# A two-layer hybrid block on one Trainium2 core: order of the routing step, arm of the expert branch, and contraction rows of the differential scores

## Chip, cores and metric

The kernel runs on one core of a Trainium2 chip. The metric is the device time of one launch in microseconds. A profiled execution gives a span from its first to its last instruction.

## What is computed

256 latent and 256 context tokens of width 1024 pass through two layers; the output is the latent stream after a last norm. All is 32-bit float. Cut to what matters here:

```python
def diff_attend(q, k, v, lam):                       # 4 heads, two score maps each
    s = jnp.einsum('bqhd,bkhd->bhqk', q, k) * HEAD_DIM ** -0.5     # HEAD_DIM = 64
    p = jax.nn.softmax(s, axis=-1).reshape(b, DIFF_HEADS, 2, nq, nkeys)
    return jnp.einsum('bhqk,bkhd->bqhd', p[:, :, 0] - lam * p[:, :, 1], v)

def moe_ffn(h, w_router, w1, w3, w2):                # layer 1, 8 experts of 3584
    top_vals, top_idx = lax.top_k(h @ w_router, 2)
    top_w = jax.nn.softmax(top_vals, axis=-1)
    gates = jnp.sum(jax.nn.one_hot(top_idx, 8) * top_w[..., None], axis=-2)
    return sum(gates[..., e:e+1] * swiglu(h, w1[e], w3[e], w2[e]) for e in range(8))

# per layer: h = modulate(rms_norm(x)); x += g_a * (concat[neighbourhood attention (4 heads),
#   differential attention, gated short conv] @ w_out); h = modulate(rms_norm(x)); x += g_f * ffn(h)
# ffn: dense SwiGLU in layer 0, moe_ffn in layer 1 (latent tokens alone)
```

## The kernel before

Activations lie transposed in SBUF (`xT`: 8 tiles of 128 features by 512 tokens; columns 256 to 511 are latent). Weights stream in over SP's queue. For the wide products a weight chunk is split into a high and a low part in fp32r (ACT writes `whi`, DVE `wlo`), and three matmuls replace one (`mm3`, lines 222 to 224).

**Mixers.** `proj_kq` projects one pair of neighbourhood heads (names `na 0`, `na 1`) or one differential head (`df 0` to `df 3`, with `rotate` set) and splits keys and queries. A score map has 64 contraction rows; `ks` and `qs` pack the high part of the keys and their low part into 128 rows, and `ql` holds the low part of the queries, one map in rows 0 to 63 and the other in rows 64 to 127. `scores` takes, for each query tile, two 128-row matmuls (line 560) and two 64-row ones (line 563); the moving side is 512 keys for latent queries, 256 for context ones. The attention itself is written as generators that two lanes step through while projections are emitted (`pace`, `step`); `finish` steps until the named heads are all emitted. The tile framework then sets each engine's order. The bias of the neighbourhood heads lies in two buffers of a pool, filled by 16 small loads a layer and masked by `mask_bias` (lines 715 and 716), on DVE for `na 0` and on GpSimd (POOL) for `na 1`.

**Routing.** After layer 1's output projection, `route` takes the norm's factor `r`, the top two experts of each token, the tokens' places in each expert (`by`, `pp`), the experts' sizes and an integer `few` for the branch. GpSimd multiplies `xT` by the norm (line 1327), ACT scales and shifts it (line 1330, the normed latents `hT`), TensorE transposes it (line 1337) into token rows `hk`, and a one-hot product gathers the rows of expert 7 from `hk` into `x7` (lines 1343 to 1347). `first_steps` then emits eight steps of expert 7 ahead of the branch: 32-column products into PSUM tiles `L` (line 1619), each step four weight chunks, with folds through PSUM tile `tg` (line 1640).

**Branch.** `moe_main` tests `few > 64`. The general arm is the larger part of the program and stands first; the data here take the other arm, which runs experts 0 and 1 as "heavy" (PSUM tiles `H`) and the others as "light" in an interleaving that a table of costs sets. Line 1903 holds the program's end and its barriers.

Of the kernel before, what the change touches and what calls it, by code (L numbers as in the profile page):

```python
# [13 lines left out]
F32 = mybir.dt.float32  # L14
F32R = mybir.dt.float32r
I32 = mybir.dt.int32
U32 = mybir.dt.uint32
# [6 lines left out]
KT = 8  # L24
# [105 lines left out]
def tile_hybrid_block(ctx: ExitStack, tc: tile.TileContext, x, c, cx, c_ctx, ada_w, ada_b, w_in, w_out, na_rpb,  # L130
# [357 lines left out]
    def proj_kq(l, name, rotate, ps=None):  # L488

        ap = st["apool"]  # L490
        q0 = 256 * l
        if ps is not None:
            pk, pq = ps
        elif l == 0:
            pk, pq = project(0, 512)
        else:
            ps = [bank("mm"), bank("mm", (128, 256))]
            for u in range(2):
                wh, wl = ws.next()
                wh = wh.rearrange("p (k n) -> p k n", k=4)  # L500
                wl = wl.rearrange("p (k n) -> p k n", k=4)
                for k in range(4):
                    kt = 4 * u + k
                    for i, a in ((0, 0), (1, 256)):
                        cs = slice(i * 128, (i + 1) * 128)
                        mm3(ps[i], wh[:, k, cs], wl[:, k, cs], hb["h"][:, kt, a:], hb["l"][:, kt, a:],
                            kt == 0, kt == KT - 1)
                    pace()
            pk, pq = ps
        units = [("na", 0), ("na", 1)] + [("df", j) for j in range(4)]  # L510
        finish(*units[:max(0, units.index(name) - 2)])

        ks = [ap.tile([128, 512], F32R, name="ks", tag="ks", bufs=6) for _ in range(2)]
        qs = [ap.tile([128, 512 - q0], F32R, name="qs", tag="qs", bufs=6) for _ in range(2)]
        ql = ap.tile([128, 512 - q0], F32R, name="ql", tag="ql", bufs=3)

        def rows_of(v):
            return v.rearrange("p (r n) -> p r n", n=GW)

        def key_parts(src, a):  # L520
            for m in range(2):
                r, o = slice(64 * m, 64 * m + 64), slice(64 - 64 * m, 128 - 64 * m)
                cs = slice(a, a + src.shape[1])
                act.activation(ks[m][r, cs], src[r], AF.Copy)
                dve.tensor_tensor(out=ks[m][o, cs], in0=src[r], in1=ks[m][r, cs].bitcast(F32), op=ALU.subtract)

        def query_parts(src, a):
            src, (hs, low) = rows_of(src), [[rows_of(q[:, a:a + src.shape[1]]) for q in qq] for qq in (qs, [ql])]
            if not rotate:

                src = src[:, :, ::-1]
            for m in range(2):
                r, o = slice(64 * m, 64 * m + 64), slice(64 - 64 * m, 128 - 64 * m)
                for h in (r, o):
                    act.activation(hs[m][h], src[r], AF.Copy, scale=0.125)
                dve.scalar_tensor_tensor(out=low[0][r], in0=src[r], scalar=0.125, in1=hs[m][r].bitcast(F32),
                                         op0=ALU.mult, op1=ALU.subtract)
        if rotate:
            uk = rope(pk[:, 256:512])
            key_parts(pk[:, :256], 0)  # L540
            uq = rope(pq[:, 256 - q0:512 - q0])
            if l == 0:
                query_parts(pq[:, :256], 0)
            key_parts(uk, 256)
            query_parts(uq, 256 - q0)
        else:
            key_parts(pk, 0)
            query_parts(pq, 0)
        st[name] = (ks, qs, ql)

    def scores(ln, kq, grp, qt, bias=None):

        ks, qs, ql = kq
        nk = 256 if grp == 0 else 512
        q0 = 256 * grp + 128 * qt - st["t0"]
        q = slice(q0, q0 + 128)
        s = [bank(f"at{ln}", (128, nk)) for _ in range(2)]
        kw = dict(skip_group_check=True)
        for m in range(2):
            pe.matmul(s[m], qs[m][:, q], ks[m][:, :nk], start=True, stop=False, **kw)  # L560
        for m in range(2):
            r = slice(64 * m, 64 * m + 64)
            pe.matmul(s[m], ql[r, q], ks[m][r, :nk], start=False, stop=True, **kw)
        if bias is not None:
            for m in range(2):
                dve.tensor_tensor(out=s[m][:, 256:], in0=s[m][:, 256:], in1=bias[m], op=ALU.add)
        return s
# [655 lines left out]
    def route():  # L1223
# [16 lines left out]
        for t in range(2):  # L1240
            for h in range(2):
# [1 line left out]
                for k in range(4):  # L1243
                    pe.transpose(p[:, k, :], xT[:, 4 * h + k, 256 + t * 128:384 + t * 128], ident)
                act.activation(xk[t][:, 4 * h:4 * h + 4, :], p, AF.Copy)
        bc = bank("mm", (128, 256))
        for t in range(2):
            pe.matmul(bc[:, t * 128:t * 128 + 128], r[:, t:t + 1].to_broadcast([128, 128]), ident, start=True,
                      stop=True)

        mo["g"] = mp.tile([128, 28 * 64], F32, name="g")
        bcs = mo["g"][:, :256]
        act.copy(bcs, bc)
        ls = mp.tile([128, 2, NE], F32, name="ls")

        by = mp.tile([128, 6, NE], F32, name="by")
        for t in range(2):
            dve.scalar_tensor_tensor(out=ls[:, t, :], in0=mo["lg"][:, t, :], scalar=r[:, t:t + 1], in1=mo["rb"],
                                     op0=ALU.mult, op1=ALU.add)
        tops, ms = [], []  # L1260
        for t in range(2):
            top, idx, idf = sm(8), sm(8, U32), sm(8)
            dve.max(out=top, in_=ls[:, t, :])
            dve.max_index(out=idx, in_max=top, in_values=ls[:, t, :])
            dve.tensor_copy(idf, idx)
            m0, m1 = sm(8), sm(8)
            dve.tensor_scalar(out=m0, in0=iota[:, :NE], scalar1=idf[:, 0:1], scalar2=None, op0=ALU.is_equal)
            dve.tensor_scalar(out=m1, in0=iota[:, :NE], scalar1=idf[:, 1:2], scalar2=None, op0=ALU.is_equal)
            dve.tensor_tensor(out=by[:, t, :], in0=m0, in1=m1, op=ALU.add)
            tops.append(top)  # L1270
            ms.append((m0, m1))
        pc = bank("at1", (128, NE))
        for t in range(2):
            pe.matmul(pc, mo["ones"], by[:, t, :], start=(t == 0), stop=(t == 1))
        pp = bank("at1", (128, 2, NE))
        pe.matmul(pp[:, 0, :], mo["before"], by[:, 0, :], start=True, stop=True)
        pe.matmul(pp[:, 1, :], mo["ones"], by[:, 0, :], start=True, stop=False)
        pe.matmul(pp[:, 1, :], mo["before"], by[:, 1, :], start=False, stop=True)
        gf = mo["gf"] = mp.tile([128, KT, 128], F32, name="gf")
        for h in range(2):  # L1280
            p = bank("mm", (128, 4, 128))
# [18 lines left out]
        mo["few"] = nc.values_load(ints[0:1, 2, 0:1], min_val=0, max_val=128 * 256)  # L1300
        dve.tensor_copy(sidf, sidx)
        for t in range(2):
            top, (m0, m1), g = tops[t], ms[t], sm(8)
            dve.tensor_scalar(out=g[:, 0:1], in0=top[:, 0:1], scalar1=-1.0, scalar2=None, op0=ALU.mult)
            act.activation(g[:, 1:2], top[:, 1:2], AF.Exp, bias=g[:, 0:1])
            dve.tensor_scalar(out=g[:, 2:3], in0=g[:, 1:2], scalar1=1.0, scalar2=None, op0=ALU.add)
# [2 lines left out]
            dve.tensor_scalar(out=by[:, 2 + t, :], in0=m1, scalar1=g[:, 4:5], scalar2=None, op0=ALU.mult)  # L1309
            dve.scalar_tensor_tensor(out=by[:, 2 + t, :], in0=m0, scalar=g[:, 3:4], in1=by[:, 2 + t, :],  # L1310
                                     op0=ALU.mult, op1=ALU.add)
        dve.tensor_copy(by[:, 4:6, :], pp)
        sel = mp.tile([128, 2, 32], F32, name="sel0")
        one_hot(sel, 0, iota[:, :32], by)

        pm = mp.tile([128, NE, NE], F32, name="pm")
        dve.tensor_tensor(out=pm, in0=iota[:, None, :NE].to_broadcast([128, NE, NE]),
# [4 lines left out]
            dve.tensor_tensor(out=pd[:, i], in0=by[:, i, None, :].to_broadcast([128, NE, NE]), in1=pm, op=ALU.mult)  # L1322
        dve.reduce_sum(out=rk, in_=pd, axis=AX.X)

        hT = mo["hT"] = xT[:, :, 256:512]
        for k in range(0, KT, 2):
            gp.tensor_tensor(out=hT[:, k:k + 2, :], in0=hT[:, k:k + 2, :],
                             in1=bcs[:, None, :].to_broadcast([128, 2, 256]), op=ALU.mult)
            for kt in (k, k + 1):
                act.activation(hT[:, kt, :], hT[:, kt, :], AF.Identity, bias=mods[1][:, 24 + kt, 1:2],  # L1330
                               scale=mods[1][:, 32 + kt, 1:2])
        hk = mo["hk"] = mp.tile([128, 2, D], F32, name="hk")
        for h in range(2):
            for t in range(2):
                p = bank("mm", (128, 4, 128))
                for k in range(4):
                    pe.transpose(p[:, k, :], hT[:, 4 * h + k, t * 128:(t + 1) * 128], ident)
                (act.copy if t else dve.tensor_copy)(hk[:, t, h * 512:(h + 1) * 512], p.rearrange("p a b -> p (a b)"))

        p = bank("mm", (128, KT, 32))  # L1340
        for t in range(2):
            for c in range(4):
                pe.matmul(p[32 * c:32 * c + 32], sel[:, t, :],
                          hk[:, t, :].rearrange("p (k c i) -> p c k i", c=4, i=32)[:, c], start=(t == 0),
                          stop=(t == 1), tile_position=(0, 32 * c), skip_group_check=True)
        x7 = mp.tile([128, KT, 32], F32, name="x7")
        dve.transpose(out=x7, in_=p)
        dstack["psum"].close()
        mo["psum"] = stack(tc.tile_pool(name="psum_m", bufs=1, space=PSUM))
        mo["rows"], mo["e"], mo["ring"] = Rows(), {}, deque()  # L1350
        mo["rows"].v["x"] = x7
        mo["fg"] = xT[:, :, 384:512]
# [12 lines left out]
        mo["left"], mo["early"] = mo["early"], {}  # L1365

    def pbank(tag):
        return mo["psum"].tile([128, 512], F32, name=tag, tag=tag, bufs={"H": 4, "L": 2, "tg": 2}[tag])

    def weights(w, r, row0, c0, nk):  # L1370

# [454 lines left out]
    def moe_main():  # L1826
        route()
        first_steps()
        with tc.If(mo["few"] > 64) as more:
            moe_general()  # L1830
        with more.Else():
            mix_experts([0, 1], [((7,), 32), ((2,), 64), ((3, 4, 5), 32)], begun=True)
# [74 lines left out]
```

## Time and profile before

| what | us |
|---|---|
| median of 3 runs | 1706.23 (1705.69 to 1714.27) |
| profiled execution, own time | 1709.09 |
| its span | 1707.3 |
| TensorE busy in it | 1639.5 (96%) |
| VectorE (DVE) / ScalarE (ACT) / GpSimd busy | 1030.1 / 639.0 / 17.6 |

TensorE is PE in the rows, its weight loads PEld. Mixer 0 lies at about 60 to 290 us of the span, the dense part up to 720, mixer 1 up to 878, routing and the first steps up to 914, the taken arm up to 1703. A matmul's busy time overlaps the next one's; what a matmul costs is read from one start to the next. A row of a window gives its start and end, its length, the busy time of PE, PEld, DVE, ACT and POOL (with the number of instructions), then TensorE's granted clock as a share of full speed, the busy share of the DMA engines, and GB/s. A row of a timeline gives start, duration, engine, line, operation, its result and inputs and their tile, size, the number of instructions joined in it, and in brackets the idle time ahead of it with what ended that.

### The profile page before, as it was taken

Reading aid. Unit: us, or ns where it says so; the run is one execution under the profiler, and the core shown is the slowest. Engines: PE = TensorE matmul, PEld = TensorE weight load, DVE = VectorE, ACT = ScalarE, POOL = GpSimd, SP = SyncE. Lnnn points to the kernel's source line nnn. Section 1 sums busy time; section 2 is a strip of 40 time slices with the busy share of each in tenths; the row PEclk is TensorE's granted clock in tenths of the full one; section 3 lists DMA queues with packets and bytes.
Section 4 is the critical chain, followed back from the end, with each engine's and each line's share of the span. In section 5 each row is a group of like instructions: output and inputs, shape, how many; then the busy total and the mean of one; then the engine's idle time right before and its main releaser. Section 6 shows DMA issues by size and latency. Waiting matters only on the chain. (4 is left out here: it accounts for less than half of the span.)

```text
span 1707.3 us, 28490 instructions
## 1 busy us (share of the span) xinstructions
PE 1639.5 (96%) x10942; PEld 1265.7 (74%) x10942; DVE 1030.1 (60%) x2043; ACT 639.0 (37%) x1057; POOL 17.6 (1%) x27
## 2 busy tenths in 40 slices
PE   7999999999999999999987999999999999999996
PEld 4777778988878888988772766676787686868773
DVE  4778877888877884788862353124454535354454
ACT  4555444422212232555533322222343234433341
POOL 0101000000000000000010000000000000000000
PEclk9999999999999999999988999999999999999999
DMA  9744343256555453352498999989999999999995
GB/s 287 179 132 111 99 149 99 88 185 197 197 169 171 154 185 111 99 149 75 162 355 312 409 380 340 349 332 401 360 368 398 364 353 364 405 386 350 388 381 193
DMA packets 234193, 434.66 MB, mean 255 GB/s; under 512 B 23496, under 2 KB 142784, under 8 KB 234048
## 3 DMA queue, kind: packets, MB, share of 16 engines
q1 hardware_dynamic: 232560, 432.14, 71.2%
q8 instruction: 88, 1.44, 0.3%
q10 hardware_dynamic: 1488, 0.62, 0.1%
q14 instruction: 57, 0.47, 0.1%
HBM read 431.66 MB, written 1.05 MB: 253 GB/s over the span
## 5 line engine op out<-in xcount | busy, mean ns | idle before, releaser
L471 DVE TENSOR_TENSOR wlo<-raw,whi 128x1024 fp32r<-128x1024 f32 x168 | 202.9, 1223 | 234.2 <-ACT whi L469 221.5
L222 PE MATMUL H<-xh,whi 128*128 128x256 f32 x896 | 257.2, 287 | 2.6 <-ACT whi L469 1.8
L224 PE MATMUL H<-xh,wlo 128*128 128x256 f32 x896 | 254.5, 284 | 2.0 <-DVE wlo L471 1.9
L223 PE MATMUL H<-xl,whi 128*128 128x256 f32 x896 | 254.1, 284 | 0.0
L469 ACT ACTIVATE whi<-raw 128x1024 fp32r<-128x1024 f32 x168 | 174.3, 1054 | 180.4 <-PE H L223 86.3
L222 PE MATMUL mm<-hh,whi 128*128 128x512 f32 (+1 forms) x648 | 230.4, 356 | 2.4 <-ACT hh L469 1.7
L223 PE MATMUL mm<-hl,whi 128*128 128x512 f32 (+1 forms) x648 | 225.8, 349 | 0.0
L224 PE MATMUL mm<-hh,wlo 128*128 128x512 f32 (+1 forms) x648 | 225.7, 349 | 0.0
L100 ACT ACTIVATE whi<-raw 128x1024 fp32r<-128x1024 f32 x130 | 134.3, 1055 | 241.4 <-DMA raw<-in_ffn_w_dram 128.2
L101 DVE TENSOR_TENSOR wlo<-raw,whi 128x1024 fp32r<-128x1024 f32 x130 | 157.0, 1221 | 60.1 <-ACT whi L100 59.3
L222 PEld LDWEIGHTS H<-xh,whi 128*128 128x128 f32 x896 | 172.3, 192 | 20.0 <-issue 9.3
L224 PEld LDWEIGHTS H<-xh,wlo 128*128 128x128 f32 x896 | 172.4, 192 | 3.0 <-DVE wlo L471 3.0
L223 PEld LDWEIGHTS H<-xl,whi 128*128 128x128 f32 x896 | 172.4, 192 | 0.2
L222 PEld LDWEIGHTS mm<-hh,whi 128*128 128x128 f32 x648 | 122.9, 190 | 22.5 <-issue 4.0
L1619 PE MATMUL L<-raw,xT 128*32 128x512 f32 (+1 forms) x896 | 137.2, 597 | 0.3
L224 PEld LDWEIGHTS mm<-hh,wlo 128*128 128x128 f32 x648 | 122.9, 190 | 16.7 <-issue 2.1
L223 PEld LDWEIGHTS mm<-hl,whi 128*128 128x128 f32 x648 | 123.3, 190 | 13.7 <-issue 0.5
L322 DVE SCALAR_TENSOR_TENSOR ada_t<-raw,scol,ada_t 128x256 f32<-128x256 f32 x266 | 116.6, 482 | 2.8
L1632 ACT ACTIVATE s<-L 128x512 f32<-128x512 f32 x70 | 41.8, 597 | 152.6 <-PE L L1619 127.2
L222 PE MATMUL H<-whi,gh 128*128 128x512 f32 x224 | 90.0, 402 | 3.9 <-ACT gh L469 3.1
L1644 DVE STREAM_TRANSPOSE sT<-tg 128x128 f32<-128x128 f32 x56 | 15.5, 308 | 129.4 <-PE tg L1640 129.3
L223 PE MATMUL H<-wlo,gh 128*128 128x512 f32 x224 | 88.8, 396 | 0.9 <-DVE wlo L471 0.9
(312 smaller groups left out, 2754.1 us busy)
## 6 DMA issues: line engine op xcount, KB each, us to landing
raw<-in_moe_w_dram SPq DMA_DIRECT2D x572, 512.0 KB, 8.3
raw<-in_ada_w_dram SPq DMA_DIRECT2D x40, 1024.0 KB, 5.2
raw<-in_ffn_w_dram SPq DMA_DIRECT2D x32, 1024.0 KB, 5.5
raw<-in_w_in_dram SPq DMA_DIRECT2D x12, 1024.0 KB, 5.2
raw<-in_w_in_dram SPq DMA_DIRECT2D x24, 512.0 KB, 5.4
aw<-in_ada_w_dram SPq DMA_DIRECT2D x16, 512.0 KB, 7.4
far<-in_moe_w_dram SPq DMA_DIRECT2D x16, 512.0 KB, 8.3
raw<-in_w_out_dram SPq DMA_DIRECT2D x5, 1024.0 KB, 5.6
```

The costliest lines, as they stand in the source:

```text
L100: self.nc.scalar.activation(hi, r, AF.Copy)
L101: self.nc.vector.tensor_tensor(out=lo, in0=r, in1=hi.bitcast(F32), op=ALU.subtract)
L222: return [pe.matmul(o, ah, bh, start=start, stop=False, **kw), pe.matmul(o, ah, bl, start=False, stop=False, **kw), pe.matmul(o, al, bh, s ...
L223: pe.matmul(o, ah, bl, start=False, stop=False, **kw),
L224: pe.matmul(o, al, bh, start=False, stop=stop, **kw)]
L322: dve.scalar_tensor_tensor(out=t[:, g, :], in0=raw[:, kt, :], scalar=scol[:, kt, g:g + 1], in1=t[:, g, :], op0=ALU.mult, op1=ALU.add)
L469: act.activation(hi, src, AF.Copy, scale=scale)
L471: dve.tensor_tensor(out=lo, in0=src, in1=hi.bitcast(F32), op=ALU.subtract)
L1619: chained(pe.matmul(o[c * n:(c + 1) * n, :], lhs, rhs, start=(k < ng), stop=(k >= nk - ng), tile_position=(0, c * n), skip_group_check=True))
L1632: act.activation(s, a, AF.Copy)
L1644: dve.transpose(out=t, in_=p)
```

## The change

1. `proj_kq` gives a differential head two `ql` tiles of 128 rows, one for each map, whose other 64 rows GpSimd sets to zero; `scores` multiplies them over 128 rows. Heads 0, 1 and 3 take these tiles from the bias buffers, and so `proj_kq` first finishes `na 0`, `na 1` and `df 0`. Neighbourhood heads keep the 64-row form.
2. In `route` the rows of expert 7 are gathered from the stream itself, with the norm's factor in the one-hot (`hit`), and scaled and shifted afterwards. The normed latents come behind that, and their product with the norm moves from GpSimd to DVE. The top-two step handles both token tiles in one instruction where it can.
3. The PSUM pool of the experts becomes three pools.
4. The branch is told that its first arm is not the one to fall through to: the other arm is laid next to it.

```diff
+        if not rotate:
+            ql = ap.tile([128, 512 - q0], F32R, name="ql", tag="ql", bufs=3)
+        else:
+            j = int(name[1])
+            if j == 2:
+                ql = [ap.tile([128, 512 - q0], F32R, name="ql", tag="ql", bufs=3) for _ in range(2)]
+            else:
+                finish(*([("na", j)] if j < 2 else [("df", 0)]))
+                t = hparts["bias"].tile([128, 2, 512], F32R, name="bias", tag="bias", bufs=2)
+                ql = [t[:, m, :512 - q0] for m in range(2)]
+            for m in range(2):
+                gp.memset(ql[m][64 - 64 * m:128 - 64 * m].bitcast(F32), 0.0)
...
         for m in range(2):
+            if isinstance(ql, list):
+                pe.matmul(s[m], ql[m][:, q], ks[m][:, :nk], start=False, stop=True, **kw)
+                continue
             r = slice(64 * m, 64 * m + 64)
             pe.matmul(s[m], ql[r, q], ks[m][r, :nk], start=False, stop=True, **kw)
...
+        hit = sm(2)
+        dve.tensor_tensor(out=hit, in0=by[:, 0:2, 0], in1=r, op=ALU.mult)
+        dve.tensor_copy(by[:, 4:6, :], pp)
+        sel = mp.tile([128, 2, 32], F32, name="sel0")
+        for t in range(2):
+            dve.tensor_scalar(out=sel[:, t, :], in0=iota[:, :32], scalar1=by[:, 4 + t, 0:1], scalar2=hit[:, t:t + 1],
+                              op0=ALU.is_equal, op1=ALU.mult)
+        p = bank("mm", (128, KT, 32))
+        for t in range(2):
+            for c in range(4):
+                pe.matmul(p[32 * c:32 * c + 32], sel[:, t, :],
+                          xk[t].rearrange("p k (c i) -> p c k i", c=4)[:, c], start=(t == 0),
+                          stop=(t == 1), tile_position=(0, 32 * c), skip_group_check=True)
+        x7 = mp.tile([128, KT, 32], F32, name="x7")
+        dve.transpose(out=x7, in_=p)
+        for s8, op in ((32, ALU.mult), (24, ALU.add)):
+            dve.tensor_tensor(out=x7, in0=x7, in1=mods[1][:, s8:s8 + 8, 1:2].to_broadcast([128, KT, 32]), op=op)
...
+        bc = bank("mm", (128, 256))
...
+        act.copy(bcs, bc)
         hT = mo["hT"] = xT[:, :, 256:512]
         for k in range(0, KT, 2):
-            gp.tensor_tensor(out=hT[:, k:k + 2, :], in0=hT[:, k:k + 2, :],
+            dve.tensor_tensor(out=hT[:, k:k + 2, :], in0=hT[:, k:k + 2, :],
                              in1=bcs[:, None, :].to_broadcast([128, 2, 256]), op=ALU.mult)
...
-        with tc.If(mo["few"] > 64) as more:
+        with tc.If(mo["few"] > 64, preferred_fallthrough_block=False) as more:
```

**TensorE at the end of `route`.** Before (`ident,xT` are the transposes, `hk,sel` the gather, `L` the first product of expert 7):

```order
L1244 MATMUL mm<-ident,xT 128x128 x16
L1248 MATMUL mm<-ident,sm 128x128 x2
L1283 MATMUL mm<-ident,mods_110 128x128 x5
L1274 MATMUL at_9039<-by,ones 128x8
L1276 MATMUL at_9042<-by,before 128x8
L1277 MATMUL at_9042<-by,ones 128x8
L1283 MATMUL mm<-ident,mods_110 128x128 x3
L1274 MATMUL at_9039<-by,ones 128x8
L1278 MATMUL at_9042<-by,before 128x8
L1337 MATMUL mm<-ident,xT 128x128 x16
L1343 MATMUL mm<-hk,sel_9106 32x256 x8
L1619 MATMUL L<-raw_8661,x_9166 32x512
```

And with the change (`xT,sel` is the gather, `ident,sm` spreads the norm's factor):

```order
L1261 MATMUL mm<-ident,xT 128x128 x16
L1284 MATMUL at_9044<-by,before 128x8
L1285 MATMUL at_9044<-by,ones 128x8
L1286 MATMUL at_9044<-by,before 128x8
L1289 MATMUL at_9048<-by,ones 128x8 x2
L1301 MATMUL mm<-xT,sel_9054 32x256 x8
L1312 MATMUL mm<-ident,mods_110 128x128 x8
L1353 MATMUL mm<-ident,sm 128x128 x2
L1369 MATMUL mm<-ident,xT 128x128 x16
L1643 MATMUL L<-raw_8679,x_9066 32x512
```

The gather moves ahead of the factor's spreading and of the second set of transposes; those 16 transposes still stand before the first `L`.

**GpSimd in the mixers.** Before, the masks of `na 1` in layer 0 and in layer 1, and then the tables of `route_early`:

```order
L184 AFFINE_SELECT flip<-flip 128x128
L715 TENSOR_TENSOR bias<-bias,mask_t 128x1024
L716 TENSOR_TENSOR bias<-bias,mask_t 128x1024
L715 TENSOR_TENSOR bias<-bias,mask_t 128x1024
L716 TENSOR_TENSOR bias<-bias,mask_t 128x1024
L1158 IOTA iota 128x256
```

With the change (the memsets are the zero halves):

```order
L732 TENSOR_TENSOR bias<-bias,mask_t 128x1024
L733 TENSOR_TENSOR bias<-bias,mask_t 128x1024
L528 MEMSET ql 64x512
L528 MEMSET bias 64x512 x2
L528 MEMSET ql 64x512
L528 MEMSET bias 64x512 x4
L732 TENSOR_TENSOR bias<-bias,mask_t 128x1024
L733 TENSOR_TENSOR bias<-bias,mask_t 128x1024
L528 MEMSET ql 64x256 x2
L528 MEMSET bias 64x256 x6
L1175 IOTA iota 128x256
```

Layer 1's mask now stands behind the memsets of layer 0's heads, whose buffers it takes over; its loads on SP's queue move likewise, behind the last scores of `df 1` and `df 3`.

**SP at the branch.** Before, the loads of the first steps end, `few` is read, and what follows the branch is the general arm:

```order
L1194 DMA far_8930<-in_moe_w_dram 128x1024
L1300 TENSOR_LOAD ints
L1300 ISA x2
L1829 COMPARE_AND_BRANCH
L1838 TENSOR_LOAD ints
L1838 ISA x2
L1839 TENSOR_LOAD ints
```

With the change what follows is the taken arm's first load:

```order
L1211 DMA far_8964<-in_moe_w_dram 128x1024
L1329 TENSOR_LOAD ints
L1329 ISA x2
L1853 COMPARE_AND_BRANCH
L1211 DMA raw_8679<-in_moe_w_dram 128x1024
L1211 DMA raw_8683<-in_moe_w_dram 128x1024
```

The same holds on every engine, and the taken arm, which stood last and ran into the program's end, now ends in a jump over the general arm. Inside the taken arm each engine has the same instructions in the same order as before. In layer 1, 49 projection matmuls instead of 120 now stand between the second scores of `na 0` and the first of `df 0`; in layer 0 the order of scores and projections hardly changes.

## Rows read from the trace of the kernel before

**Rows 1.** Windows of the span (columns told under the table above).

```profile
138.00:264.00 126.00, 120.22 (x687) 90.51 (x684) 103.48 (x276) 63.22 (x149) 4.85 (x2) 0.97 0.38 117
...
776.00:830.00 54.00, 52.50 (x355) 46.00 (x354) 48.69 (x114) 28.98 (x59) 0.00 (x0) 1.00 0.29 96
...
1020.00:1100.00 80.00, 80.00 (x465) 50.38 (x464) 22.48 (x29) 18.04 (x27) 0.00 (x0) 1.00 0.91 339
```

**Rows 2.** Timeline of TensorE, mixer 0: start, us, what; a 64-row matmul alone.

```profile
214.26 0.40 PE L560 MATMUL at<-ks,qs 128*128 128x512 f32 x1
214.58 0.50 PE L563 MATMUL at<-ks,ql 64*128 64x512 f32 x1
215.01 0.50 PE L224 MATMUL mm<-hh,wlo 128*128 128x512 f32 x1
215.35 0.40 PE L222 MATMUL mm<-hh,whi 128*128 128x512 f32 x1
```

**Rows 3.** The same in mixer 1: a pair of them.

```profile
788.25 0.49 PE L563 MATMUL at<-ks,ql 64*128 64x512 f32 x2
788.67 0.50 PE L222 MATMUL mm<-hh,whi 128*128 128x512 f32 x1
789.01 0.39 PE L223 MATMUL mm<-hl,whi 128*128 128x512 f32 x1
789.24 0.40 PE L224 MATMUL mm<-hh,wlo 128*128 128x512 f32 x1
```

**Rows 4.** Timeline of GpSimd, layer 1's mask (its second half follows).

```profile
140.97 2.40 POOL L715 TENSOR_TENSOR bias<-bias,mask_t 128x1024 f32<-128x1024 f32 x1 [70.03 <-DMA bias<-in_na_rpb_dram]
```

**Rows 5.** Line 536 on DVE: duration ns min/median/max, first and last start.

```profile
L536 DVE SCALAR_TENSOR_TENSOR ql<-rope_u,qs x16: 406/422/2156, 123.3 to 821.7; 64x256 fp32r<-64x256 f32 x16
```

**Rows 6.** Timeline of TensorE, mixer 0: in brackets its idle time before.

```profile
152.38 0.63 PE L580 MATMUL at<-ident,p 128*128 128x128 f32 x4 [3.02 <-DVE p L638]
```

**Rows 7.** Timeline of TensorE, mixer 1: scores of `na 0`, its transposes.

```profile
748.84 0.49 PE L563 MATMUL at<-ks,ql 64*128 64x512 f32 x2
...
762.88 0.61 PE L580 MATMUL at<-flip,p 128*128 128x128 f32 x4
```

**Rows 8.** Timeline of `route`, in order of time, all engines.

```profile
882.17 4.94 POOL L1327 TENSOR_TENSOR xT<-xT,g 128x512 f32<-128x512 f32 x4 [25.64 <-ACT g L1253]
882.26 1.20 DVE L1269 TENSOR_TENSOR by<-sm 128x8 f32<-128x8 f32 x1
...
887.17 0.17 DVE L1269 TENSOR_TENSOR by<-sm 128x8 f32<-128x8 f32 x1
...
890.01 2.55 ACT L1330 ACTIVATE xT<-xT,mods 128x256 f32<-128x256 f32 x5
...
893.87 1.94 PE L1343 MATMUL mm<-hk,sel 128*32 128x256 f32 x16 [0.57 <-DVE hk L1338]
...
896.38 4.93 PE L1619 MATMUL L<-raw,x 128*32 128x512 f32 x36 [0.57 <-DVE x L1347]
```

**Rows 9.** Line 1829, the branch: instruction, ns min/median/max, start.

```profile
L1829 PEldq COMPARE_BRANCH x1: 6056/6056/6056, 914.9 to 914.9; - x1
...
L1829 ACTq EVENT_SEMAPHORE x1: 17/17/17, 1703.5 to 1703.5; - x1
```

**Rows 10.** Waits of SP's queue, 896 to 940 us: total, times, longest.

```profile
SPq L1903 <- SPq L1903: 5.5, 1, 5.5
```

**Rows 11.** Timeline of TensorE across the branch.

```profile
913.67 0.43 PE L1640 MATMUL tg<-s,fold 128*32 128x128 f32 x8 [0.43 <-ACT s L1632]
921.19 2.74 PE L1619 MATMUL L<-raw,x 128*32 128x512 f32 x9 [7.09 <-ACT xh L469]
...
926.36 1.92 PE L1619 MATMUL L<-raw,x 128*32 128x512 f32 x16
```

**Rows 12.** A window across the branch, columns as in the first group.

```profile
914.10:926.40 12.30, 4.88 (x26) 1.52 (x29) 4.07 (x10) 2.19 (x4) 0.00 (x0) 0.72 0.63 239
```

**Rows 13.** Line 1903, the program's end: ns min/median/max, first and last start.

```profile
L1903 SPq DRAIN x3: 7/7/13, 1706.5 to 1706.9; - x3
```

More of the change, by code (lines that the diff above doesn't have):

```diff
@@ L514, in proj_kq @@
         qs = [ap.tile([128, 512 - q0], F32R, name="qs", tag="qs", bufs=6) for _ in range(2)]
-        ql = ap.tile([128, 512 - q0], F32R, name="ql", tag="ql", bufs=3)
+        if not rotate:
[10 more added lines that the diff above has]
+                gp.memset(ql[m][64 - 64 * m:128 - 64 * m].bitcast(F32), 0.0)
         def rows_of(v):
@@ L527, in query_parts @@
         def query_parts(src, a):
-            src, (hs, low) = rows_of(src), [[rows_of(q[:, a:a + src.shape[1]]) for q in qq] for qq in (qs, [ql])]
+            src, (hs, low) = rows_of(src), [[rows_of(q[:, a:a + src.shape[1]]) for q in qq]
+                                            for qq in (qs, ql if rotate else [ql, ql])]
             if not rotate:
@@ L535, in query_parts @@
                     act.activation(hs[m][h], src[r], AF.Copy, scale=0.125)
-                dve.scalar_tensor_tensor(out=low[0][r], in0=src[r], scalar=0.125, in1=hs[m][r].bitcast(F32),
+                dve.scalar_tensor_tensor(out=low[m][r], in0=src[r], scalar=0.125, in1=hs[m][r].bitcast(F32),
                                          op0=ALU.mult, op1=ALU.subtract)
@@ L1245, in route @@
                 act.activation(xk[t][:, 4 * h:4 * h + 4, :], p, AF.Copy)
[L1246 to L1249, printed above, removed]
         mo["g"] = mp.tile([128, 28 * 64], F32, name="g")
-        bcs = mo["g"][:, :256]
-        act.copy(bcs, bc)
         ls = mp.tile([128, 2, NE], F32, name="ls")
@@ L1259, in route @@
                                      op0=ALU.mult, op1=ALU.add)
-        tops, ms = [], []
+        tops = mp.tile([128, 2, NE], F32, name="tops")
+        idx = mp.tile([128, 2, NE], U32, name="idx")
+        idf = mp.tile([128, 2, NE], F32, name="idf")
+        ms = [mp.tile([128, 2, NE], F32, name=f"m{i}") for i in range(2)]
         for t in range(2):
[L1262 to L1274, printed above, removed]
+            dve.max(out=tops[:, t, :], in_=ls[:, t, :])
+            dve.max_index(out=idx[:, t, :], in_max=tops[:, t, :], in_values=ls[:, t, :])
+        dve.tensor_copy(idf, idx)
+        for i in range(2):
+            dve.tensor_tensor(out=ms[i], in0=iota[:, None, :NE].to_broadcast([128, 2, NE]),
+                              in1=idf[:, :, i:i + 1].to_broadcast([128, 2, NE]), op=ALU.is_equal)
+        dve.tensor_tensor(out=by[:, 0:2, :], in0=ms[0], in1=ms[1], op=ALU.add)
         pp = bank("at1", (128, 2, NE))
@@ L1278, in route @@
         pe.matmul(pp[:, 1, :], mo["before"], by[:, 1, :], start=False, stop=True)
+        pc = bank("at1", (128, NE))
+        for t in range(2):
+            pe.matmul(pc, mo["ones"], by[:, t, :], start=(t == 0), stop=(t == 1))
+        hit = sm(2)
[6 more added lines that the diff above has]
+        p = bank("mm", (128, KT, 32))
+        for t in range(2):
+            for c in range(4):
[6 more added lines that the diff above has]
+            dve.tensor_tensor(out=x7, in0=x7, in1=mods[1][:, s8:s8 + 8, 1:2].to_broadcast([128, KT, 32]), op=op)
         gf = mo["gf"] = mp.tile([128, KT, 128], F32, name="gf")
@@ L1302, in route @@
         for t in range(2):
-            top, (m0, m1), g = tops[t], ms[t], sm(8)
+            top, m0, m1, g = tops[:, t, :], ms[0][:, t, :], ms[1][:, t, :], sm(8)
             dve.tensor_scalar(out=g[:, 0:1], in0=top[:, 0:1], scalar1=-1.0, scalar2=None, op0=ALU.mult)
@@ L1311, in route @@
                                      op0=ALU.mult, op1=ALU.add)
-        dve.tensor_copy(by[:, 4:6, :], pp)
-        sel = mp.tile([128, 2, 32], F32, name="sel0")
-        one_hot(sel, 0, iota[:, :32], by)
         pm = mp.tile([128, NE, NE], F32, name="pm")
@@ L1323, in route @@
         dve.reduce_sum(out=rk, in_=pd, axis=AX.X)
+        bc = bank("mm", (128, 256))
+        for t in range(2):
+            pe.matmul(bc[:, t * 128:t * 128 + 128], r[:, t:t + 1].to_broadcast([128, 128]), ident, start=True,
+                      stop=True)
+        bcs = mo["g"][:, :256]
+        act.copy(bcs, bc)
         hT = mo["hT"] = xT[:, :, 256:512]
         for k in range(0, KT, 2):
-            gp.tensor_tensor(out=hT[:, k:k + 2, :], in0=hT[:, k:k + 2, :],
+            dve.tensor_tensor(out=hT[:, k:k + 2, :], in0=hT[:, k:k + 2, :],
                              in1=bcs[:, None, :].to_broadcast([128, 2, 256]), op=ALU.mult)
@@ L1338, in route @@
                 (act.copy if t else dve.tensor_copy)(hk[:, t, h * 512:(h + 1) * 512], p.rearrange("p a b -> p (a b)"))
[L1340 to L1347, printed above, removed]
         dstack["psum"].close()
-        mo["psum"] = stack(tc.tile_pool(name="psum_m", bufs=1, space=PSUM))
+        mo["psum"] = {t: stack(tc.tile_pool(name=f"psum_{t}", bufs=1, space=PSUM)) for t in ("H", "L", "tg")}
         mo["rows"], mo["e"], mo["ring"] = Rows(), {}, deque()
@@ L1367, in pbank @@
     def pbank(tag):
-        return mo["psum"].tile([128, 512], F32, name=tag, tag=tag, bufs={"H": 4, "L": 2, "tg": 2}[tag])
+        return mo["psum"][tag].tile([128, 512], F32, name=tag, tag=tag, bufs={"H": 4, "L": 2, "tg": 2}[tag])
     def weights(w, r, row0, c0, nk):
```

## Prediction

> **What bounds the kernel now.** I read the windows first. Over the whole span TensorE is busy 96%, but a mean tells nothing of a stage, so I took three stretches. In the middle of mixer 0 TensorE is busy 120.2 of 126 us and VectorE 103.5; in mixer 1, 52.5 of 54 and 48.7; in the taken arm of the branch 80.0 of 80, with the DMA at 0.91 of its time [rows 1]. So the mixers wait for TensorE with VectorE close behind, and in the arm TensorE sets the pace while the DMA is nearly full. Time taken off TensorE in mixer 0 mostly passes to the end; in mixer 1 less surely; in the arm nothing is changed, so what is won or lost ahead of it passes through, if its weights keep up. Then I read timelines of TensorE around the matmuls that change, and last of the routing step and the branch.
>
> **Scores over 128 rows.** Look at starts, not durations. Alone, the sequence 128-row, 64-row, 128-row, 128-row starts at 214.26, 214.58, 215.01 and 215.35: steps of 0.32, 0.43 and 0.34 us [rows 2], where neighbouring 128-row matmuls of that size step by 0.23 (789.01 to 789.24) [rows 3]. One lone 64-row matmul thus costs 0.09 + 0.20 + 0.11 = 0.40 more than a 128-row one. A pair is different: two take 0.42 together, no longer than one alone, so the two halves of the array do run side by side; but the step behind them is 0.34 again [rows 3] and the step ahead loses some 0.09, so a pair costs about 0.42 + 0.11 + 0.09 against 2 x 0.23, an excess of 0.16. The matmul itself gains from 64 rows; entering and leaving the form costs more than it gains.
>
> The Trainium skill (TensorEngine Tiling (Array Packing), Theoretical Speedup) gives up to twice the rate for products of 64 rows or fewer that are tiled by rows, which speaks against this change. The trace agrees for the pair itself and not for the whole; by that rule alone the change would add 0.23 a pair, and it is the third rival below.
>
> The differential heads of mixer 0 have 18 lone ones and 7 pairs: 18 x 0.40 + 7 x 0.16 = 8.3 us. Mixer 1 has 10 and 3, half as long on the moving side for some: 4.5. In mixer 0 TensorE is the busier by far and I let 0.7 of it pass: **-6** (0 to -8.3). In mixer 1 VectorE is busy 90% of the stretch [rows 1], and something is added there, so I take nothing for the scores alone.
>
> **The moved mask.** GpSimd's mask of layer 1 runs from 140.97, 2.40 us each half [rows 4]. Under it, one of VectorE's operations on line 536 took 2156 ns instead of 422 [rows 5], and TensorE then waited 3.02 us for VectorE at 152.38 [rows 6] and ran some microseconds behind it with less clock (the window's mean is 0.97 [rows 1]; some 1.7 us by it). That is 4.7 us that goes. The two halves now run after the last scores of `df 3`, near the end of mixer 0, where VectorE has the last attention's norm to do and could be held for as long: 0 to +4.8, and where TensorE has dense weights to work on it costs less. With part of it coming back: **-2** (-4.7 to +1.8 for this and the memsets). SP's bias loads wait longer at its queue's head, until those buffers are free; the weights behind them belong to the dense part, and I take 0.
>
> **Finishing heads early.** `finish` before a differential head leaves only 49 projection matmuls to cover the chain from the last scores of `na 0` to the first of `df 0` in mixer 1. That chain, scores to transposes, takes 748.84 to 762.88, 14.0 us [rows 7], most of it queueing behind VectorE. 49 matmuls at 0.23 cover 11.3, which leaves TensorE some 3 us bare, and the next head's a little. This eats the 4.5 of the scores: **0** for mixer 1 together, from -4.5 to +9 (two chains, each bare for another 6). In mixer 0 the order hardly changes: 0. The zero halves are memsets on an idle GpSimd, which is busy for 4.85 us of the 126 [rows 1]: 0, with what they may cost VectorE among the mask's bounds.
>
> **The routing step.** Before, GpSimd's product starts at 882.17 and is busy 4.94 us; VectorE's small operation goes from 0.17 to 1.20 us beside it, so `by` is ready only at 887.3, and the first product of expert 7 starts at 896.38 [rows 8]. With the change GpSimd is out, `by` comes at about 882.4, the places and the one-hot 1.0 to 1.4 later, the gather ends 1.0 to 1.9 after that (it took 1.94 [rows 8]), near 885.7. But the order of TensorE puts ten small matmuls and sixteen transposes between it and the first `L`: ten at 0.16 (four take 0.63 [rows 6]), 1.6; one copy by ACT, 0.5; one product on VectorE, 0.6 (an estimate from 0.42 for a quarter of it [rows 5], with headroom by its fixed part); eight ACT operations at 2.55 / 5 = 0.51 [rows 8], 4.1; the last transposes 0.7 to 1.2. That is 885.7 + 1.6 + 0.5 + 0.6 + 4.1 + 1.0 = 893.5, or 894.3 with a handover of 0.1 to each of the steps: 2.1 earlier. What TensorE has to wait for in between lowers its clock as now, which I charge with 0.6: **-1.5** (0 to -3). The gathered rows themselves are early; they wait for the transposes in front of them.
>
> **The branch.** TensorE's compare-and-branch takes 6056 ns from 914.9 [rows 9], SP's 5.5 us [rows 10]; TensorE is idle 7.09 us before 921.19 [rows 11], and from 914.10 to 926.40 its mean granted clock is 0.72, between the two levels of 1.2 and 2.4 GHz [rows 12]. So the jump costs the stall and then slow matmuls. From 914.10 to the next step's start at 926.36 are 12.3 us in which it does one step and the tail of the step before. One step at full clock takes 1.92 [rows 11], the tail about 0.7 (folds of 0.43 [rows 11] and a handover), reading the integer and an untaken branch 0.8 (no row prices these: an estimate from the 7.09 idle less the 6.06). 12.3 - 3.4 = 8.9; with a little kept back, **-8.7** (-5.5, the stall alone with the slow clock left, to -9).
>
> The Trainium skill (Runtime: NRT & Kernel Launch, Instruction fetch mechanics) says that instructions are fetched ahead in sequence only, and that a taken branch to somewhere outside what is fetched waits for the fetch. The trace agrees for the taken one with its 6056 ns; no run before shows one that falls through.
>
> **The jump at the end.** The taken arm stood last and ran into the program's end; now each engine jumps over the general arm there. ACT's last step of the arm is at 1703.5 [rows 9]; with the jump it arrives at 1703.5 + 5.5 = 1709.0 (SP's price [rows 10]), against 1706.5 when SP finds the last output written [rows 13]. The other 3 us lie beside that transfer: **+2.5** (0 to +5.5, where SP itself jumps only after its last wait).
>
> **Sum.** -6 + 0 - 2 - 1.5 - 8.7 + 2.5 = -15.7 on the profiled execution's own 1709.1, 1693.4. That execution is 2.9 above the median of the runs, 1706.2, so on the median's scale **1690.5**. Inside the arm all instructions stand in the same order, and the stock of weights at its start is smaller by what TensorE no longer waits; at 940 and after TensorE did not wait for them, and I take 0.
>
> **The rivals.**
> *The weight of the two mixers doesn't pass* (VectorE bounds them: its 103.5 of 126, 48.7 of 54). For: its queue is what the 14.0 us chain is made of. Then -7.7 of routing, branch and end is left: 1698.5, no measurable change by a hair.
> *The arm next to the branch isn't reached cheaply* (it falls through, but its code is not there yet, so the fetch stands where the jump stood). For: no row shows one. Against: the straight stretches of the rows pay nothing like it. It gives back 8.7: 1699.2, no change.
> *64 rows side by side* are worth more than their entry: if the step losses of rows 2 belong to something else, 128 rows cost 0.23 more a pair of 512 and 0.12 of 256, some +4.6 in place of -6, so about 1701. Against: every lone one shows the loss.
> *Finishing early makes it slower.* If no projection covers the chain of `na 0` and of `na 1` in mixer 1, both 14.0 us [rows 7], and VectorE's queue doesn't shorten, TensorE stands 28 us there: +28 against the -15.7, so 1718. It decides from 15.7 us bare; at 24 it is slower by the bound below. For: the chain's length. Against: 49 matmuls stand in the first, and with fewer heads at once VectorE's queueing shrinks.
> *More than forecast*: all of both mixers' TensorE time passes, 3 of the routing, nothing lost at the end: -6.8 - 2.5 - 1.5 - 2.7 beyond, about 1677.
>
> **How the numbers follow.** The forecast, with its own range of 1683 to 1697, has 0.66; more than that 0.06; the three that end near 1698 to 1701 have 0.24 (0.10, 0.09 and 0.05); the slower one 0.04. About 0.5%, 8.5 us, is what a measurement of this kernel can tell from no change: below 1697.7 is faster (0.72), to 1714.8 the same (0.24), above it slower (0.04). The range leaves out the far end on each side: 1683 to 1702.
>
> **What would show it.** Right: differential scores over 128 rows step by 0.23 with no loss around them, and losses only at the neighbourhood heads; no compare-and-branch above 1 us, no gap at 905 to 915 and full clock behind it; the first `L` 2 us sooner after the last output projection; the slow VectorE rows of 141 gone and some near the end of mixer 0; a stall of 5 us on each engine at the program's end. Wrong: TensorE idle for more than 6 us in mixer 1 at 750 to 790; a fetch at the branch all the same; TensorE waiting for weights in the taken arm from 940 on.

## The result, and the profile after

The changed kernel took 1693.8 us, median of 4 runs, against 1707.5 for the kernel before (4 runs beside it): a ratio of 0.990 (0.987 to 0.992). Forecast were 1690.5, in a range of 1683 to 1702. The profiled execution took 1694.6 (span 1692.8), 14.5 less than the one of before.

Comparing busy shares says little (TensorE has 96% in both). I cut both executions at marks that the two have in common instead, starts of TensorE's instructions, and let each stretch speak for itself. The first is a wait of 1.59 us for a split weight in mixer 0, then the sums of the norms before the dense part and before routing, the first `L`, the first heavy product, the last heavy product. Mixer 1 is counted from the first matmul behind the dense part. The dense part took 411.4 to 411.6 us in every kernel of this study and is left out below.

| stretch, us | before | after | difference | forecast |
|---|---|---|---|---|
| start to the mark in mixer 0 | 81.3 | 84.6 | +3.4 | 0 |
| mixer 0 from there | 221.9 | 215.4 | -6.5 | -8 |
| mixer 1 | 163.1 | 157.8 | -5.3 | 0 |
| routing to the first `L` | 18.6 | 18.4 | -0.2 | -1.5 |
| first steps and branch to the first heavy product | 37.8 | 28.6 | -9.2 | -8.7 |
| from there to the last heavy product | 748.0 | 749.5 | +1.5 | 0 |
| to the end of the span | 25.2 | 27.0 | +1.8 | +2.5 |

The windows that answer to [rows 1], moved with the work, and the one that answers to [rows 12]:

```profile
134.80:260.80 126.00, 120.41 (x739) 94.54 (x738) 108.02 (x298) 66.95 (x160) 1.35 (x2) 1.00 0.42 125
772.80:826.80 54.00, 52.28 (x361) 47.53 (x361) 50.31 (x116) 29.67 (x58) 0.61 (x2) 1.00 0.29 98
1001.70:1081.70 80.00, 80.00 (x464) 50.28 (x463) 22.58 (x29) 17.85 (x26) 0.00 (x0) 1.00 0.92 348
904.70:917.00 12.30, 9.10 (x92) 3.18 (x88) 5.96 (x16) 7.24 (x13) 0.00 (x0) 1.00 1.04 395
```

In the mixers TensorE is busy as long as before for more work: in mixer 0 739 matmuls in place of 687, at a clock of 1.00 in place of 0.97. The arm is unchanged. Behind the branch the clock is 1.00 in place of 0.72, with 9.1 us of TensorE's work in place of 4.9.

A differential score on TensorE's timeline, to be held against [rows 2]:

```profile
184.63 0.50 PE L574 MATMUL at<-ks,qs 128*128 128x512 f32 x1
184.97 0.39 PE L577 MATMUL at<-ks,bias 128*128 128x512 f32 x1
185.19 0.39 PE L222 MATMUL mm<-hh,whi 128*128 128x512 f32 x1
185.42 0.39 PE L223 MATMUL mm<-hl,whi 128*128 128x512 f32 x1
```

The low product and the one behind it step by 0.22 and 0.23. The step ahead of the low product is still 0.34 here, but this place is an exception, as e2 shows below.

The branch, by instruction, and TensorE's timeline across it (held against [rows 9] and [rows 11]):

```profile
L1853 ACTq COMPARE_BRANCH  x2: 38/44/49, 904.7 to 1688.0; - x2
L1853 PEldq COMPARE_BRANCH  x2: 95/1738/3382, 905.6 to 1678.9; - x2
```

```profile
904.31 0.42 PE L1664 MATMUL tg<-s,fold 128*32 128x128 f32 x8 [0.41 <-ACT s L1656]
905.91 1.92 PE L1643 MATMUL L<-raw,x 128*32 128x512 f32 x16 [1.17 <-DMA raw<-in_moe_w_dram]
907.76 0.44 PE L1461 MATMUL tg<-ident,sel 128*128 128x128 f32 x2
```

Each row of the first fence joins two instructions: on TensorE, 95 ns is the branch that falls through, 3382 ns the new jump at the arm's end. The idle 7.09 us of before are 1.17 here, and what ends them is a load of weights. The program's end, to be held against [rows 13]:

```profile
L1927 SPq DRAIN  x3: 7/7/13, 1692.0 to 1692.3; - x3
...
L1927 ACTq DRAIN  x2: 8/37/66, 1691.9 to 1692.3; - x2
```

ACT jumps at 1688.0 and arrives at 1691.9, no later than SP. Routing, all engines, to be held against [rows 8]:

```profile
876.06 1.91 PE L1301 MATMUL mm<-xT,sel 128*32 128x256 f32 x16 [0.63 <-DVE sel L1296]
...
877.90 2.83 PE L1312 MATMUL mm<-ident,mods 128*128 128x128 f32 x16
...
880.57 0.61 PE L1353 MATMUL mm<-ident,sm 128*128 128x128 f32 x4
...
881.26 0.37 ACT L1356 COPY g<-mm 128x256 f32<-128x256 f32 x1
881.66 0.69 DVE L1359 TENSOR_TENSOR xT<-xT,g 128x512 f32<-128x512 f32 x1 [0.65 <-ACT g L1356]
882.39 4.12 ACT L1362 ACTIVATE xT<-xT,mods 128x256 f32<-128x256 f32 x8 [0.76 <-DVE xT L1359]
883.04 3.96 PE L1369 MATMUL mm<-ident,xT 128*128 128x128 f32 x16 [1.86 <-ACT xT L1362]
...
887.72 0.64 PE L1643 MATMUL L<-raw,x 128*32 128x512 f32 x4 [0.72 <-ACT hk L1370]
```

The gather ends at 877.97; the first `L` waits 9.7 us longer, for transposes that it doesn't need and for the last copy out of their PSUM tiles.

### The profile page after: what moved, and what is told of

It is laid out like the page before. It is cut to its first block, busy times and chain, and to the rows that moved or that the text cites. A ratio compares the mean times of both kernels' runs of the same rounds, so it can differ in the third digit from the quotient of the medians.

```text
span 1692.8 us, 28521 instructions
## 1 busy us (share of the span) xinstructions
PE 1628.5 (96%) x10942; PEld 1266.0 (75%) x10942; DVE 1025.3 (61%) x2046; ACT 639.9 (38%) x1057; POOL 20.6 (1%) x39
## 5 line engine op out<-in xcount | busy, mean ns | idle before, releaser
L471 DVE TENSOR_TENSOR wlo<-raw,whi 128x1024 fp32r<-128x1024 f32 x168 | 202.9, 1222 | 233.7 <-ACT whi L469 221.9
```

The source lines that it names most:

```text
L471: dve.tensor_tensor(out=lo, in0=src, in1=hi.bitcast(F32), op=ALU.subtract)
```

## The experiments

All are measured against the kernel before, as ratios of medians; the changed kernel has 0.990 on that scale. The stretches are those of the table above, from the profiled execution of each.

| kernel | ratio (95%) | mixer 0 | mixer 1 | to first `L` | to first heavy | arm | end |
|---|---|---|---|---|---|---|---|
| e1 general arm first | 0.995 (0.994 to 0.997) | 216.5 | 158.3 | 18.3 | 41.9 | 749.5 | 25.8 |
| e2 64 rows | 0.995 (0.994 to 0.997) | 223.6 | 159.0 | 19.5 | 28.5 | 747.9 | 26.3 |
| e3 old heads | 0.996 (0.994 to 0.997) | 222.4 | 162.6 | 19.9 | 30.2 | 749.2 | 27.0 |
| e5 old heads, finishing early | 0.996 (0.994 to 0.997) | 227.7 | 159.1 | 18.5 | 28.6 | 749.5 | 26.9 |
| e6 mask on VectorE | 0.990 (0.988 to 0.992) | 214.6 | 156.3 | 19.7 | 28.5 | 748.0 | 26.3 |
| e8 norm's product on GpSimd | 0.991 (0.990 to 0.993) | 217.3 | 156.9 | 21.1 | 31.1 | 748.1 | 26.3 |
| e4 late rows | 0.989 (0.986 to 0.992) | 214.9 | 157.7 | 14.8 | 30.8 | 747.9 | 26.2 |
| e7 late all | 0.988 (0.986 to 0.990) | 213.1 | 157.7 | 12.1 | 34.6 | 749.4 | 27.0 |

The changed kernel, e1, e4 and e8 are the same up to the end of mixer 1 and show how far one execution repeats: mixer 0 214.9 to 217.3 (mean 216.0), mixer 1 156.9 to 158.3 (157.7). Up to the first mark they took 84.6, 81.4, 81.1 and 82.3, so the 3.4 us that the changed kernel lost there are that execution's, not the change's. Routing is the same in the changed kernel, e1, e2, e3, e5 and e6, and takes 18.3 to 19.9 to the first `L`, so there one execution doesn't tell a difference of 1.5 us. The three PSUM pools, the gather from the stream and the joined top-two step were not tested by themselves.

**e1, the arm's place.**

```diff
-        with tc.If(mo["few"] > 64, preferred_fallthrough_block=False) as more:
+        with tc.If(mo["few"] > 64) as more:
```

> The changed kernel with the general arm first again at the branch, all else kept. If the layout is what the branch's 8.5 us came from: TensorE's compare-and-branch is back at some 6 us, the first heavy product lies 8 to 9 us after its place in the changed kernel as counted from the last fold ahead of the branch, the program's end is about 1 us shorter, and the whole is 6 to 9 us slower than the changed kernel, near 1701. If the arm is paced by its weights and takes back what is won ahead of it: the branch is slower by as much, but the whole by less than 3 us.

The ratio is 0.56% above the changed kernel's, 9.6 us. TensorE's rows at the branch:

```profile
L1853 PEldq COMPARE_BRANCH  x1: 6156/6156/6156, 903.9 to 903.9; - x1
```

```profile
910.20 1.92 PE L1643 MATMUL L<-raw,x 128*32 128x512 f32 x5 [7.14 <-ACT xh L469]
913.62 3.62 PE L1643 MATMUL L<-raw,x 128*32 128x512 f32 x11 [1.50 <-issue]
```

The stall is back, with a second stop of 1.50 behind it and a clock of 0.50 from 912 to 920, and the first heavy product lies 13 us later, more than either theory had (this execution is 3.5 us above e1's median); the end is 1.2 shorter. The arm doesn't take it back: the theory that it does falls, and so does the prediction's rival of an arm that isn't reached cheaply.

**e2, 64 rows, and e3, the old heads.** e2 changes one line; e3 puts `proj_kq` and `scores` back as they were.

```diff
-                pe.matmul(s[m], ql[m][:, q], ks[m][:, :nk], start=False, stop=True, **kw)
+                r = slice(64 * m, 64 * m + 64)
+                pe.matmul(s[m], ql[m][r, q], ks[m][r, :nk], start=False, stop=True, **kw)
```

> The changed kernel with the low products of the differential scores over 64 rows again, of the same zero-padded tiles (early finishing, zero halves and moved masks kept). If entering and leaving the 64-row form costs 0.3 to 0.4 us for a lone one and TensorE bounds the mixers: mixer 0 ends 4 to 7 us later than in the changed kernel, mixer 1 adds 2 to 5, the whole is 6 to 10 us slower. If VectorE bounds the mixers: TensorE works 8 us longer there and waits less, and the whole is less than 3 us slower. If two 64-row matmuls side by side are worth more than the form: the whole is faster.

> The changed kernel with the heads of the kernel before, one low tile for both maps, no early finishing, the masks where they were. The traces put mixer 0 at -3.2 and mixer 1 at -5.3 us, so this is 8 to 9 us slower than the changed kernel if nothing outside the mixers answers to them. If finishing early and the moved mask cost what the scores don't pass on (the forecast had 10.5 us of gain in mixer 0): it is faster than the kernel with 64 rows alone by 3 us or more, most of it in mixer 0. If they cost nothing: the same as that one within 1.5 us.

e2 is 0.56% above the changed kernel, 9.6 us; its mixer 0 is 7.6 longer than the mean, its mixer 1 only 1.3. In both mixers the two kernels run the same matmuls in the same order, so their traces can be laid side by side, start by start. One place in the changed kernel, then the same place in e2:

```profile
179.53 0.39 PE L574 MATMUL at<-ks,qs 128*128 128x512 f32 x1
179.76 0.39 PE L577 MATMUL at<-ks,bias 128*128 128x512 f32 x1
179.98 0.39 PE L222 MATMUL mm<-hh,whi 128*128 128x512 f32 x1
180.21 0.39 PE L223 MATMUL mm<-hl,whi 128*128 128x512 f32 x1
```

```profile
178.42 0.39 PE L574 MATMUL at<-ks,qs 128*128 128x512 f32 x1
178.74 0.50 PE L578 MATMUL at<-ks,bias 64*128 64x512 f32 x1
179.17 0.51 PE L222 MATMUL mm<-hh,whi 128*128 128x512 f32 x1
179.51 0.40 PE L223 MATMUL mm<-hl,whi 128*128 128x512 f32 x1
```

The three steps are 0.23, 0.22 and 0.23, and in e2 0.32, 0.43 and 0.34: 0.41 more. Over all of mixer 0, e2's steps ahead of low products are 2.4 us longer in sum (longer at 25 of 29 places), their own 4.3 and those behind 1.7. That makes 8.4, as much as the 8.2 by which e2's mixer 0 is above that of the changed kernel's execution. What else differs cancels: e2 waits longer near 270 us, with a slow clock behind it,

```profile
269.39 0.58 PE L222 MATMUL at<-pth,vh 128*128 128x256 f32 x1 [2.70 <-ACT pth L469]
```

where the changed kernel waits 1.32, and less elsewhere. In mixer 1 the steps make 3.6 and 1.2 are left; the clock takes part of it back (0.83 from 828 to 838 us in the changed kernel, 1.00 in the same stretch of e2). So the form is what the scores gain, and in mixer 0 as much as all of it passes. Side-by-side halves are not worth their entry. The Trainium skill (TensorEngine Tiling (Array Packing), Key Properties) says that changing the tiling mode drains TensorE. The trace agrees: the steps around a lone 64-row product are longer by the amounts above, and over 128 rows they are not. e3 is the same as e2 in total, as the last of its theories has it, but not stage by stage: mixer 0 is 1.2 shorter, mixer 1 3.7 longer.

**e5, finishing early alone**, on e3:

```diff
+        if rotate and name[1] != 2:
+            finish(*([("na", int(name[1]))] if int(name[1]) < 2 else [("df", 0)]))
         ql = ap.tile([128, 512 - q0], F32R, name="ql", tag="ql", bufs=3)
```

> The changed kernel with the heads of the kernel before (one low tile, 64-row products, masks where they were) and only the early finishing left in. The kernel with old heads took 162.6 us for mixer 1, the one with 64-row products but early finishing and zero halves 159.0. If finishing early is what took the difference: mixer 1 is 159 to 160 here, without the waits of 1.7 and 1.3 us and the slow clock some 120 us into it. If it is the zero halves, the moved loads or the buffers: mixer 1 stays at 162 to 163. In mixer 0 the mask of layer 1 is where it was before, so its wait of 3 us at 152 is back.

Mixer 1 falls from 162.6 to 159.1, where e2 has 159.0: it is the finishing. The windows that show it, 110 to 130 us into mixer 1, of e3 and then of e2:

```profile
825.08:845.08 20.00, 16.95 (x95) 13.61 (x93) 16.64 (x43) 9.48 (x21) 0.00 (x0) 0.83 0.69 260
```

```profile
826.47:846.47 20.00, 19.02 (x131) 15.90 (x130) 19.40 (x54) 10.21 (x23) 0.00 (x0) 1.00 0.60 233
```

With the old order TensorE waits there twice, and its clock is down to 1.2 GHz for a while; the kernel before shows the same waits (1.73 and 1.33), and in e5 the clock of that stretch is 1.00 as in e2. In e3:

```profile
834.77 0.35 PE L222 MATMUL mm<-hh,whi 128*128 128x256 f32 x1 [1.72 <-ACT hh L469]
...
836.46 0.90 PE L583 MATMUL at<-ident,p 128*128 128x128 f32 x3 [1.33 <-DVE p L641]
```

In mixer 0 the same call costs 5.3 (222.4 to 227.7): there is a wait of 2.00 at 94 us that e3 doesn't have, the one at 153 is 3.74 in place of 2.99, and from 140 to 180 the clock is 0.87 in place of 0.96. The order of the scores changes too: of the 64-row products of mixer 0, 30 stand alone and 5 in pairs in e5, 20 and 10 in e3, which costs with 64 rows and not with 128. From e5 to e2, which moves the mask and adds the zero halves, mixer 0 gets 4.1 back; the wait at 153 is gone. Finishing, mask and zero halves together are e2 less e3, +1.2.

**e6, the mask on VectorE** in layer 1.

```diff
-        e = gp if u else dve
+        e = gp if u and st["t0"] == 0 else dve
```

> The changed kernel with layer 1's mask of na 1 on VectorE, in mixer 1, in place of GpSimd at the end of mixer 0. If the moved mask holds VectorE there: the 2.2 us operation of the norm is back at 0.16, TensorE's waits near 265 and 275 us (1.3 and 1.8 us) go, and mixer 0 is 2 to 3.5 us shorter from the same mark; mixer 1 pays 0 to 1.5 us for 2.4 us more on VectorE. If these waits are the attention's own: mixer 0 is the same within 0.7 us.

In the changed kernel the moved mask holds one small operation of the norm on VectorE, and TensorE waits for that norm:

```profile
268.15 3.29 POOL L732 TENSOR_TENSOR bias<-bias,mask_t 128x1024 f32<-128x1024 f32 x1 [110.65 <-DVE p L655]
...
271.70 2.24 DVE L235 TENSOR_TENSOR sm<-sm 128x2 f32<-128x2 f32 x1
...
275.56 0.71 PE L673 MATMUL at<-ident,sm 128*128 128x128 f32 x4 [1.76 <-DVE sm L237]
```

In e6 the operation takes 0.16 and the wait is gone; the one near 265 stays at 1.19 and is the attention's own. Mixer 0 is 1.4 below the mean, which one execution doesn't settle, and the total is the same. e7 below has the same edit and a mixer 0 of 213.1; both lie below all four of the others, so some 2 us is likely but not shown.

**e8, the norm's product on GpSimd** (line 1359, `gp` for `dve`).

> The changed kernel with the latents' product with the norm on GpSimd again, where the changed order has it. GpSimd took 1.24 us for each of four parts against VectorE's 0.69, so the first product of expert 7 comes 1.5 to 3 us later, and the whole with it if the weights don't hide that. If the harm was in what GpSimd did to VectorE's routing steps, which are now ahead of it: no more than that, and the small VectorE operations of the top-two step stay at 0.17 us.

The first `L` comes 2.7 us later than in the changed kernel (1.2 to 2.8 later than in the six with its routing), the total is 0.15% higher with overlapping intervals, and the top-two step keeps its 0.17 us. Moving the product off GpSimd pays for the later place that the change gives it; its place behind the gather is what frees the top-two step.

**e4, late rows, and e7, late all.** e4 puts the transposes behind the first steps:

```diff
+        def token_rows(h):
+            for t in range(2):
+                p = pbank("H").rearrange("p (a b) -> p a b", a=4)
...
+        mo["between"] = deque([lambda: (normed(0), normed(2)), lambda: (normed(4), normed(6)),
+                               lambda: token_rows(0), lambda: token_rows(1)])
...
             next(run)
+            if mo["between"]:
+                mo["between"].popleft()()
```

> The changed kernel with the normed latents and their sixteen transposes behind the first steps of expert 7, in PSUM tiles of the experts, so that the first product of expert 7 has only the gather ahead of it. If those transposes hold it: it starts 5 to 7 us earlier (about 881.5 us of the span in place of 887.7), and the first heavy product and the end come 3 to 6 us earlier. If the weights then hold it: it starts as early, TensorE waits for a DMA of weights between 885 and 905, and the first heavy product and the end come less than 1.5 us earlier.

> The kernel with late normed latents, with three more edits: the spreading of the gate factors also behind the first steps, the norm's factor spread early as in the kernel before, and layer 1's mask of na 1 on VectorE. The first product of expert 7 has only the gather ahead: about 10 us after the norm's sum (14.8 with late rows alone, 18.4 in the changed kernel). If TensorE's own work sets the pace up to the first heavy product: that comes 3 to 5 us earlier than in the changed kernel, and with the mask the whole is 4 to 7 us faster than it. If the weights set it: the first heavy product comes less than 1.5 us earlier, with waits for DMA before it, and the whole is 1.5 to 3.5 us faster through the mask.

The first `L` comes 3.6 and 6.3 us sooner after the norm's sum, the first heavy product 1.4 and 0.3. Neither theory is whole: the only wait for weights is the one of the changed kernel (1.08 in place of 1.17 us). What is gained in waiting goes to the transposes, which now stand between steps (2.4 us in e4), and in e7 to the clock: its first 48 products of expert 7 take 7.80 us where the changed kernel's take 5.51. (Five of the transposes also came ahead of the first `L` in e7, so that it took 12.1 us and not the 10 expected.)

```profile
875.33 7.80 PE L1650 MATMUL L<-raw,x 128*32 128x512 f32 x48
```

The window of that stretch has the clock at 0.75:

```profile
875.00:885.00 10.00, 10.00 (x81) 2.87 (x83) 3.62 (x21) 3.75 (x7) 0.00 (x0) 0.75 1.03 407
```

e7 is the fastest kernel here by its median (1687.5); its interval overlaps the changed kernel's.

## Why the prediction was right, and where its terms were off

**The scores.** The mechanism is right, and the 0.40 for a lone product of 512 columns too (0.41). That the sum came out (8.3 counted, 8.4 measured) is partly luck: I counted 18 lone ones and 7 pairs in the old order, and the changed order has 26 and 3; and I gave those of 256 columns the same price, where all 26 have a mean of about 0.30. In mixer 1 the steps are 3.6, not 4.5. Of the two shares that I let pass, 0.7 in mixer 0 should have been nearly 1 (e2 less the mean: 7.6), and nothing in mixer 1 should have been 1.3.

**Finishing early** is the step that failed, both ways. I took the chain of `na 0` to be bare for 3 us in mixer 1; TensorE doesn't wait more there, and a later pair of waits with slow clock goes: -3.5 (e5 less e3) for a forecast that spent 4.5. In mixer 0, where I read hardly a change of order and took 0, it costs 5.3 with the old heads and the mask in its old place (e5 less e3); in the changed kernel it can't be told from the mask.

**The mask**: 4.1 gained for the mask and the zero halves together in mixer 0 (e5 to e2), net of what comes later; in the changed kernel that is the 1.8 us wait that e6 removes. Forecast -2, within its bounds of -4.7 to +1.8. Against the old heads, though, finishing, mask and zero halves together are +1.2 in mixer 0, where my terms have -2: the scores alone make that mixer's gain.

**Routing**: -0.2 for -1.5, and with 18.3 to 19.9 for the same step in six kernels no gain is shown. I counted 7.8 us from the gather's end to the first `L`, and it is 9.7: the spreading of gates and norm takes 3.3 (877.90 to 881.18) where I had 1.6. The trace counts 16 and 4 matmuls where the order has 8 and 2, and the clock is down for most of the first 2 us of it:

```profile
877.90:879.90 2.00, 2.00 (x14) 2.00 (x11) 1.84 (x12) 0.03 (x1) 0.00 (x0) 0.59 1.03 418
```

The last copy out of PSUM stood in no term. The gather's end itself comes 8.6 us after the norm's sum, where I had 7.9.

**The branch**: -9.2 for -8.7, 0.7 of it the first steps' own clock. The Trainium skill (Runtime: NRT & Kernel Launch, Instruction fetch mechanics) has a taken branch wait for the fetch of a target that isn't fetched yet. The trace agrees: 95 ns for the branch that falls through, and 6156 for the same one taken in e1.

**The end**: +1.8 for +2.5, less by e6 and e8 (+1.1). e1, which has no jump there, has +0.6, so the jump itself is worth 0.5 to 1.2. ACT's jump took 3.9, not 5.5. Of the signs named beforehand two didn't show: a first `L` 2 us sooner (0.2) and a stall of 5 us at the end (3.4 on TensorE, 3.9 on ACT).

**In the arm** I took 0. A wait of 1.55 us stands near its end in both kernels; in the changed one the clock is 0.89 for 16 us around it, in the one before 1.00:

```profile
1644.00:1660.00 16.00, 14.09 (x81) 8.19 (x81) 4.96 (x8) 3.03 (x5) 0.00 (x0) 0.89 0.78 294
```

The same stretch of the kernel before:

```profile
1661.97:1677.97 16.00, 14.09 (x92) 8.35 (x92) 4.95 (x8) 3.62 (x6) 0.00 (x0) 1.00 0.85 322
```

0.11 of 16 us is some 1.7 us, and e2, e4, e6 and e8, at 747.9 to 748.1, don't pay it.

Put together: -15.7 forecast; mixer 1 gave 5.3 more, the branch 0.5 and the end 0.7; mixer 0 gave 1.5 less, routing 1.3, the arm 1.5, and the start cost 3.4 by chance: -14.5. So the branch came out by its mechanism, and the mixers' sum (-11.8 for -8) by terms that missed in both directions. That the whole lies 1.2 us from the forecast sum is in part luck.

## What to carry to other kernels

A matmul over half the rows, alone between full ones, can cost more than the same one padded with zeros: look at the steps of its neighbours, and undo it on one line to know. Where a branch nearly always goes one way, lay that arm next to it, and count the stall with the slow clock behind it. A product that is ready early gains nothing while unrelated transposes stand ahead of it on its engine; and moving those away pays only for the waiting, not for the work.

## What was not expected of the hardware

The same wait of 1.55 us near the arm's end, in the same instructions, leaves the clock at 1.00 in six of these ten executions (before, e2, e3, e4, e6, e8) and brings it to 0.89 in four (the changed kernel, e1, e5, e7); a microsecond or two between such kernels needs no other cause. The jump over the general arm at the end took 3.4 us on TensorE and 3.9 on ACT, where TensorE's at the branch had taken 6.1. GpSimd's mask held a VectorE operation of two elements on each of 128 partitions for 2.24 us, where it takes 0.16.
